# A fused encoder block on one core: the large SBUF tiles moved to multiples of 2 KiB

## The chip, the core and the metric

The kernel runs on one core of a Trainium2 chip. The metric is the device time of one execution in microseconds. TensorE is written PE, its weight loads PEld; VectorE is DVE, ScalarE is ACT, GpSimd is POOL, and SP is the engine whose queue issues most of the DMAs.

## What is computed

One residual block of an encoder on x of 256 rows by 2048 columns, float32, with all weights streamed from HBM once:

```python
h      = rmsnorm(x, g_mix)
proj   = h @ w_in                       # 2048 x 10240: q,k,v twice, two gates
y_sb   = stick_breaking_attention(...)  # 8 heads of 128
y_ca   = chunked_relpos_attention(...)  # 8 heads of 128
x = x + (sigmoid(gate_sb) * (y_sb @ w_sb_out)
         + sigmoid(gate_ca) * (y_ca @ w_ca_out)) @ w_mix_out
h = rmsnorm(x, g_ffn);  g, u = split(h @ w_ffn_in)      # 2048 x 11264
x = x + (silu(g) * u) @ w_ffn_out                       # 5632 x 2048
h = rmsnorm(x, g_ple)
x = x + sigmoid(h @ w_ple_gate) * (p @ w_ple_in)
out = rmsnorm(x, g_final)
```

## The kernel before

**Splitting.** Each float32 operand of a product is split into a rounded part (hi) and a remainder (lo), both float32r, and a product takes three partial products: hi·hi, hi·lo, lo·hi. A piece of 512 KB of weights lands in one of five `raw` buffers; ACT rounds it into `hi` (L173) and DVE subtracts into `lo` (L174), each of three buffers. The activations lie split as well, in tables `T1`, `T2` and `T3` of shape [128, 16, 2, 256]: for each of 16 blocks of the contraction, 256 columns hi and 256 columns lo, 2 KiB in a row.

**Two kinds of product.** A "feat" piece holds four contraction blocks of 256 weight columns. For each block and each half of the columns PE loads 128 columns of `hi` and streams all 512 columns of the table (hi and lo, L198), then loads 128 columns of `lo` and streams the 256 hi columns (L200). I call these two matmuls, 512 and 256 columns, a *pair*. A "row" piece holds two contraction blocks of 512 weight columns; there the table is loaded as weights and 512 columns of `hi` or `lo` are streamed, three matmuls for each block and row half (L181 to L183). In each pair the weights and the streamed table are two different SBUF tiles:

```python
    nc.tensor.matmul(ps, hi[:, i, f], lhs[:, kt, :, :].rearrange("p c s -> p (c s)"),
                     start=a, stop=False)                                        # L198
    nc.tensor.matmul(ps[:, :S], lo[:, i, f], lhs[:, kt, 0, :], start=False, stop=z)  # L200
```

The first argument after the output is loaded as weights, the second is streamed; in `row_products` it is the table that is loaded.

**Stages in order of time.** v of the first four heads and p @ w_ple_in as row pieces (to 51 us, the second with the small table `pT`); then q, k and v of both mixers with the attention worked in between, and both gates, all on T1 (to 504 us); w_sb_out and w_ca_out on T2 (to 594 us); w_mix_out on T1 (to 685 us); then three blocks of w_ffn_in on T3 followed by w_ffn_out on T2, T1 and T2 (T3: 685 to 864, 955 to 1133 and 1224 to 1358 us; T2: 865 to 955 us; T1: 1134 to 1224 us; T2: from 1358 us); last w_ple_gate as row pieces with T1 as weights, its last 512 columns kept split in T2 and T3, and the final norm.

**Order of work.** A list of pieces is worked in order; loads are issued five pieces ahead by SP (L158), splits two ahead, and small tasks (attention, norms) run between pieces. The framework then schedules the instructions of each engine and puts in the semaphores.

**Where the tiles lie.** A pool's tiles lie one behind the other in the order of their first use, each rounded up to 32 bytes, and pools lie behind each other in the order in which they are opened. The offset of a tile in a partition, modulo 2048, before the change: the framework's own constants take the first 128 bytes, so T1, T2 (32 KiB each) and xT (16 KiB) lie at 128. The small constants after them take 4640 bytes (ident 512, ones 512, mhalf 32, gT 192, rbc 1024, three rstd 96, sqs 2048, three ms 96, msq 64, rest 32, rfin 32), so all that follows lies 4640 bytes further, at 672: `raw`, `hi`, `lo` (4 KiB a buffer), v, qT and kT, and T3, which later takes the place of v. A block of 128 weight columns is 512 bytes, so weights out of `hi` and `lo` start at 160 modulo 512, streamed slices of T1 and T2 at 128 and those of T3 at 160. In row pieces the weights out of T1 start at 128 modulo 512, those out of pT (at 1696) at 160, and the streamed `hi` and `lo` at 160. All these numbers are read from the program's allocation.

Of the kernel before, what the change touches and what calls it, by code (L numbers as in the profile page):

```python
# [9 lines left out]
F32 = mybir.dt.float32  # L10
F32R = mybir.dt.float32r
# [5 lines left out]
P = 128  # L17
S = 256
NT = 2
D = 2048  # L20
KD = D // P
# [19 lines left out]
def block_kernel(ctx: ExitStack, tc: tile.TileContext, x, p, w_in, w_sb_out, w_ca_out, w_mix_out,  # L41
# [12 lines left out]
    outr = out[0].rearrange("(t p) d -> p t d", p=P)  # L54

    cp = ctx.enter_context(tc.tile_pool(name="const", bufs=1))
    wp = ctx.enter_context(tc.tile_pool(name="wts", bufs=1))
    dp = ctx.enter_context(tc.tile_pool(name="dram", bufs=1, space=bass.MemoryType.DRAM))
    ps_mm = ctx.enter_context(tc.tile_pool(name="ps_mm", bufs=4, space=PSUM))
# [7 lines left out]
    def const(name, shape, dt=F32):  # L67
        return cp.tile(shape, dt, tag=name, name=name)

    T1 = const("T1", [P, KD, 2, S], F32R)  # L70
    T2 = const("T2", [P, KD, 2, S], F32R)
    xT = const("xT", [P, KD, S])


    ident = const("ident", [P, P])
# [50 lines left out]
    def group(kind, wsrc, n0, kts, lhs, post, needs=lambda kt: None, row0=0, keep=None):  # L126

        ncol, nk = (NB, 2) if kind == "row" else (FB, 4)
        g = dict(kind=kind, post=post, lhs=lhs, ps=None, keep=keep)
        kts = list(kts)  # L130
        for j in range(0, len(kts), nk):
            part = kts[j : j + nk]
            r = (row0 + j) * P
            pieces.append(dict(
                g=g, kts=part, ncol=ncol, first=j == 0, last=j + nk >= len(kts),
                src=wsrc[r : r + len(part) * P, n0 : n0 + ncol].rearrange("(k p) n -> p k n", p=P),
                needs=[k for k in (needs(kt) for kt in part) if k is not None],
            ))
# [78 lines left out]
    def flush(every=1):  # L217

        while state["at"] < len(pieces):
            pc = pieces[state["at"]]  # L220
            prefetch()
            products(pc)
            state["at"] += 1
            if tasks and state["at"] % every == 0:
                run_task()
# [40 lines left out]
    def x_tiles(kt, ps):  # L266
# [5 lines left out]
        for k in range(n):  # L272
            g = gT[:, kt + k : kt + k + 1]
            hi = T1[:, kt + k, 0, :]
            if k == 0:
                nc.scalar.activation(hi, ps[:, k, :], AF.Identity, scale=g)
            else:
                nc.vector.tensor_scalar(hi, ps[:, k, :], g, None, ALU.mult)
            nc.vector.scalar_tensor_tensor(T1[:, kt + k, 1, :], ps[:, k, :], g, hi.bitcast(F32),
                                           ALU.mult, ALU.subtract)  # L280
# [40 lines left out]
    def v_tile():  # L321
        return mp.tile([P, NT, NB], F32, tag="v", name="v")

    def scale_v(v, ps):
        for t in range(NT):
            nc.scalar.activation(v[:, t, :], ps[t], AF.Identity, scale=rstd["mix"][:, t : t + 1])
# [12 lines left out]
    v0 = v_tile()  # L339
    group("row", w2, 2 * W, range(KD), T1, lambda ps: tasks.append(("v", lambda: scale_v(v0, ps))), needs=hneed)  # L340
    for c in range(4):
# [40 lines left out]
    def feat_post(dst, h0, sc, then):  # L382
        def post(ps):
            for f in range(2):
                sm = halves(ps[f], mp)
                if sc is None:
                    nc.vector.tensor_tensor(dst[:, h0 + f, :], sm, rbc, ALU.mult)
                else:
                    nc.vector.scalar_tensor_tensor(dst[:, h0 + f, :], sm, sc, rbc, ALU.mult, ALU.mult)
            if then is not None:  # L390
                then()
        return post

    def split_y(ps, kt):
        src = ps[:, :512].rearrange("p (k s) -> p k s", k=2)
        nc.scalar.copy(T2[:, kt : kt + 2, 0, :], src)
        nc.vector.tensor_tensor(T2[:, kt : kt + 2, 1, :], src, T2.bitcast(F32)[:, kt : kt + 2, 0, :], ALU.subtract)
        done.add(("y", kt))
# [133 lines left out]
    def push_attention(s1, s2, s3):  # L532
        for s, h in ((s1, 0), (s2, 0), (s3, 0), (s1, 2), (s2, 2), (s3, 2)):
            tasks.append((None, lambda s=s, h=h: s(h)))

    for mixer, make in ((0, sb_tasks), (1, ca_tasks)):
        for b in range(2):
# [5 lines left out]
            if not first:  # L543
                group("row", w2, c0 + 2 * W, range(KD), T1, lambda ps, v=v: scale_v(v, ps), needs=hneed)
            for dst, off, sc in ((qT, 0, SCALE), (kT, W, None)):
                for j in range(2):
                    then = None
                    if off and j == 1:
                        then = lambda t=make(qT, kT, v, 4 * b): push_attention(*t)
                    group("feat", w2, c0 + off + j * FB, range(KD), T1, feat_post(dst, 2 * j, sc, then), needs=hneed)  # L550
            flush(4)

    def gate_post(m, j):
        def post(ps):
            for f in range(2):
                sm = halves(ps[f], mp)
                nc.vector.tensor_tensor(gates[:, m, 2 * j + f, :], sm, rbc, ALU.mult)
        return post

    for j in range(8):  # L560
        for m in range(2):
            group("feat", w2, 6 * W + m * D + j * FB, range(KD), T1, gate_post(m, j), needs=hneed)
    flush(4)

    def out_post(m, j):
        def post(ps):
            gt = gates[:, m, 2 * j : 2 * j + 2, :]
            nc.scalar.activation(gt, gt, AF.Sigmoid)
            for f in range(2):
                kt = 2 * j + f  # L570
                sm = halves(ps[f], mp)
                nc.vector.tensor_tensor(gates[:, m, kt, :], sm, gates[:, m, kt, :], ALU.mult)
            if m == 1:
                for kt in (2 * j, 2 * j + 1):
                    mg = gates[:, 0, kt, :]
                    nc.gpsimd.tensor_tensor(mg, mg, gates[:, 1, kt, :], ALU.add)  # L576
                    put_split(T1, kt, mg)
        return post

    for j in range(8):  # L580
        for m, wo in ((0, w_sb_out), (1, w_ca_out)):
            group("feat", wo[0], j * FB, range(8 * m, 8 * m + 8), T2, out_post(m, j),
                  needs=lambda kt: ("y", kt))
# [65 lines left out]
    for blk, nk in enumerate(FF_BLOCKS):  # L649
        dst = (T2, T1, T2)[blk]  # L650
        for i in range(0, nk, 2):
# [73 lines left out]

    keep = [t.rearrange("p k c s -> p (k c s)") for t in (T2, T3)]

# [44 lines left out]
```

## Time and profile before

| | us |
|---|---|
| median of 3 runs | 1529.45 (1529.27 to 1530.86) |
| the profiled execution | 1530.86 |
| its span, first to last instruction | 1529.2 |
| PE busy in the span | 1512.1 |

"PE busy" is the time in which at least one matmul is under way. Matmuls overlap in the profile (each is shown until its results are out), so the pace of PE is read from the distance of two starts and not from a matmul's duration.

### The profile page before, as it was taken

To read this page: it belongs to the slowest core of one execution; us is meant where nothing else is said; L and a number is where in the kernel's file an instruction comes from. 1 tells how busy PE (TensorE), PEld (TensorE's weight loads), DVE (VectorE), ACT (ScalarE), POOL (GpSimd) and SP (SyncE) were. 2 spreads that over 40 slices of the span, in tenths; PEclk is the share of its full clock that TensorE was granted. 3 is DMA by queue.
4 is the path that set the end of the run, shared out by engine and by line. 5 is a ranking of instruction groups with operands and counts; after the bars stand their busy time and mean duration, and the time that the engine had idled before them with its cause. 6 is when DMAs were issued, how large, how long until landed. Compare 5 with 4: busy or idle time off the path is not lost.

```text
span 1529.2 us, 21785 instructions
## 1 busy us (share of the span) xinstructions
PE 1512.1 (99%) x8454; PEld 1307.7 (86%) x8454; DVE 993.6 (65%) x1361; ACT 735.5 (48%) x1001; POOL 131.5 (9%) x118
## 2 busy tenths in 40 slices
PE   8999999999999999999999999999999999999997
PEld 6888888888888888888888888888888888888886
DVE  7566666666555777676666655666665566668575
ACT  5455554555444455454444433444443344445542
POOL 6300000000000122111000000000000000001100
PEclk9999999999999999999999999999999999999999
DMA  8775556555565556656565555656655566655563
GB/s 267 254 222 165 171 173 180 179 174 171 182 190 184 187 187 202 227 185 185 187 193 185 188 192 181 192 186 187 192 188 185 186 187 192 185 184 194 167 215 116
DMA packets 265174, 289.27 MB, mean 189 GB/s; under 512 B 9040, under 2 KB 244864, under 8 KB 264816
## 3 DMA queue, kind: packets, MB, share of 16 engines
q1 hardware_dynamic: 262912, 278.96, 57.7%
q0 software_dynamic: 2160, 8.93, 1.8%
q8 instruction: 66, 1.08, 0.3%
q14 instruction: 36, 0.29, 0.1%
HBM read 282.09 MB, written 5.77 MB: 188 GB/s over the span
## 4 chain that ended last, share of the span: by engine, by line
PE 96%; POOL 1%; DMA 1%; issue 1%; DVE 0%; ACT 0%; SPq 0%; POOLq 0%; DVEq 0%; ACTq 0%
PE mm L198 56%; PE mm L200 28%; PE mm L181 3%; PE mm L182 3%; PE mm L183 3%; DMA raw<-in_w_in 1%; POOL sqs L94 1%; POOL sq L292 1%; PE x2p L672 0%; PE yp L430 0%; PE wt L521 0%; PE zp L421 0%; PE yp L421 0%; PE yp L420 0%; PE zp L419 0%
## 5 line engine op out<-in xcount | busy, mean ns | idle before, releaser
L198 PE MATMUL mm<-T,hi 128*128 128x512 f32 x3648 | 1277.0, 396 | 0.0
L200 PE MATMUL mm<-T,lo 128*128 128x256 f32 x3648 | 1006.6, 280 | 0.0
L174 DVE TENSOR_TENSOR lo<-raw,hi 128x1024 fp32r<-128x1024 f32 (+1 forms) x517 | 642.4, 1243 | 416.6 <-ACT hi L173 411.1
L173 ACT CAST hi<-raw 128x1024 fp32r<-128x1024 f32 (+1 forms) x517 | 541.5, 1048 | 584.3 <-PE mm L198 435.1
L198 PEld LDWEIGHTS mm<-T,hi 128*128 128x128 f32 x3648 | 677.8, 188 | 156.0
L200 PEld LDWEIGHTS mm<-T,lo 128*128 128x128 f32 x3648 | 686.9, 188 | 8.8
L231 ACT COPY tm<-mm 128x256 f32<-128x256 f32 x184 | 68.7, 373 | 125.6 <-PE mm L200 125.6
L233 DVE TENSOR_TENSOR sm<-mm,tm 128x256 f32<-128x256 f32 x184 | 77.3, 420 | 53.9 <-ACT tm L231 53.9
L634 POOL TENSOR_TENSOR tg<-tg,sg 128x512 f32<-128x512 f32 x22 | 39.6, 1800 | 619.4 <-ACT sg L633 619.4
L182 PE MATMUL mm<-lo,T 128*128 128x512 f32 x224 | 88.9, 400 | 0.0
L183 PE MATMUL mm<-hi,T 128*128 128x512 f32 x224 | 87.7, 398 | 0.0
L181 PE MATMUL mm<-hi,T 128*128 128x512 f32 x224 | 84.5, 403 | 0.0
L182 PEld LDWEIGHTS mm<-lo,T 128*128 128x128 f32 x224 | 42.2, 189 | 9.8 <-DVE lo L174 0.4
L181 PEld LDWEIGHTS mm<-hi,T 128*128 128x128 f32 x224 | 42.2, 190 | 9.7
L183 PEld LDWEIGHTS mm<-hi,T 128*128 128x128 f32 x224 | 42.1, 189 | 9.8
L576 POOL TENSOR_TENSOR gates<-gates 128x256 f32<-128x256 f32 x16 | 19.9, 1246 | 291.2 <-ACT hi L173 280.7
L94 POOL TENSOR_TENSOR sqs<-sqs,sq 128x512 f32<-128x512 f32 x21 | 30.9, 1473 | 117.6 <-ACT sq L613 117.3
L607 DVE TENSOR_TENSOR xT<-mm,xT 128x256 f32<-128x256 f32 x64 | 25.0, 424 | 10.9 <-PE mm L200 10.9
L243 DVE SCALAR_TENSOR_TENSOR T<-xT,gT,T 128x256 fp32r<-128x256 f32 x32 | 29.4, 958 | 0.0
L608 DVE TENSOR_TENSOR xT<-mm,xT 128x256 f32<-128x256 f32 x64 | 23.9, 415 | 0.0
L489 POOL DMA_DIRECT2D bias<-ext_d x8 | 4.3, 541 | 200.8 <-DVE sl L414 161.2
L643 DVE TENSOR_TENSOR sm<-sm,rbc 128x256 f32<-128x256 f32 x44 | 18.7, 425 | 1.5
(172 smaller groups left out, 629.9 us busy)
## 6 DMA issues: line engine op xcount, KB each, us to landing
raw<-in_w_ffn_in SPq DMA_DIRECT2D x176, 512.0 KB, 3.5
raw<-in_w_in SPq DMA_DIRECT2D x159, 512.0 KB, 3.6
raw<-in_w_ffn_out SPq DMA_DIRECT2D x88, 512.0 KB, 3.4
raw<-in_w_mix_out SPq DMA_DIRECT2D x32, 512.0 KB, 3.4
raw<-in_w_ple_gate SPq DMA_DIRECT2D x32, 512.0 KB, 4.2
raw<-in_w_sb_out SPq DMA_DIRECT2D x16, 512.0 KB, 3.3
raw<-in_w_ca_out SPq DMA_DIRECT2D x16, 512.0 KB, 3.4
raw<-in_w_ple_in SPq DMA_DIRECT2D x4, 512.0 KB, 5.0
```

The costliest lines, as they stand in the source:

```text
L94: nc.gpsimd.tensor_tensor(sqs, sqs, sq, ALU.add)
L173: nc.scalar.copy(hi[:, c : c + m], raw[:, c : c + m])
L174: nc.vector.tensor_tensor(lo[:, c : c + m], raw[:, c : c + m], hi.bitcast(F32)[:, c : c + m], ALU.subtract)
L181: nc.tensor.matmul(ps, xh, hi, start=a, stop=False)
L182: nc.tensor.matmul(ps, xh, lo, start=False, stop=False)
L183: nc.tensor.matmul(ps, xl, hi, start=False, stop=z)
L198: nc.tensor.matmul(ps, hi[:, i, f], lhs[:, kt, :, :].rearrange("p c s -> p (c s)"), start=a, stop=False)
L200: nc.tensor.matmul(ps[:, :S], lo[:, i, f], lhs[:, kt, 0, :], start=False, stop=z)
L231: nc.scalar.copy(tm, ps[:, S:])
L233: nc.vector.tensor_tensor(sm, ps[:, :S], tm, ALU.add)
L243: nc.vector.scalar_tensor_tensor(dst[:, kt, 1, :], src, g, dst.bitcast(F32)[:, kt, 0, :], ALU.mult, ALU.subtract)
L634: nc.gpsimd.tensor_tensor(tg, tg, sg, ALU.mult)
```

## The change

It opens a pool `big` behind the pool of constants and moves T1, T2 and xT into it; the constants, now first, get an unused tile `fill` of 344 floats (1376 bytes) ahead of them. 128 + 1376 + 4640 = 6144 = 3 · 2048, so T1, T2 and xT lie at multiples of 2 KiB, and with them everything behind: `raw`, `hi`, `lo`, v, qT, kT and T3 move from 672 to 0 modulo 2048, pT to 1024. No instruction is added, removed or changed in its operands' shapes.

```diff
     cp = ctx.enter_context(tc.tile_pool(name="const", bufs=1))
+    bp = ctx.enter_context(tc.tile_pool(name="big", bufs=1))
     wp = ctx.enter_context(tc.tile_pool(name="wts", bufs=1))
...
-    T1 = const("T1", [P, KD, 2, S], F32R)
-    T2 = const("T2", [P, KD, 2, S], F32R)
-    xT = const("xT", [P, KD, S])
+
+    const("fill", [P, 344])
+    T1 = bp.tile([P, KD, 2, S], F32R, tag="T1", name="T1")
+    T2 = bp.tile([P, KD, 2, S], F32R, tag="T2", name="T2")
+    xT = bp.tile([P, KD, S], F32, tag="xT", name="xT")
```

## Rows read from the trace of the kernel before

**Rows 1.** The page: its first line, PE's busy time with its share and count of instructions, the granted clock in 40 slices (9 is 90% or more of full speed), and the chain of work that ended last by engine.
```profile
span 1529.2 us, 21785 instructions
...
PE 1512.1 (99%) x8454; PEld 1307.7 (86%) x8454; DVE 993.6 (65%) x1361; ACT 735.5 (48%) x1001; POOL 131.5 (9%) x118
...
PEclk9999999999999999999999999999999999999999
...
PE 96%; POOL 1%; DMA 1%; issue 1%; DVE 0%; ACT 0%; SPq 0%; POOLq 0%; DVEq 0%; ACTq 0%
```

**Rows 2.** What PE waited for, from the view of the waits of PE: us in total, times, longest.
```profile
PE gps L263 <- DMA gm<-in_g_mix: 3.5, 1, 3.5
PE nps L102 <- POOL sqs L99: 2.4, 1, 2.4
PE xps L271 <- DMA xt<-in_x: 2.0, 1, 2.0
```

**Rows 3.** The largest groups of PE by shape: count, busy us, mean ns of one.
```profile
L198 PE MATMUL mm<-T,hi 128*128 128x512 f32 x3648 | 1277.0, 396 | 0.0
L200 PE MATMUL mm<-T,lo 128*128 128x256 f32 x3648 | 1006.6, 280 | 0.0
L182 PE MATMUL mm<-lo,T 128*128 128x512 f32 x224 | 88.9, 400 | 0.0
L183 PE MATMUL mm<-hi,T 128*128 128x512 f32 x224 | 87.7, 398 | 0.0
L181 PE MATMUL mm<-hi,T 128*128 128x512 f32 x224 | 84.5, 403 | 0.0
L181 PE MATMUL mm<-hi,pT 128*128 128x512 f32 x16 | 7.0, 435 | 0.0
```

**Rows 4.** Line 198 in six stretches, one row for each: count of matmuls, duration min/median/max, and the us in which the first and the last one started. In order: gates on T1, w_sb_out and w_ca_out on T2, w_mix_out on T1, and w_ffn_out on T2, T1 and T2.
```profile
L198 PE MATMUL mm<-T,hi x349: 392/395/402, 380.7 to 503.6; 128*128 128x512 f32 x175
...
L198 PE MATMUL mm<-T,hi x256: 392/397/402, 503.9 to 594.0; 128*128 128x512 f32 x128
...
L198 PE MATMUL mm<-T,hi x256: 392/396/402, 594.4 to 684.5; 128*128 128x512 f32 x128
...
L198 PE MATMUL mm<-T,hi x256: 389/392/402, 864.7 to 954.6; 128*128 128x512 f32 x128
...
L198 PE MATMUL mm<-T,hi x255: 392/395/402, 1134.2 to 1224.0; 128*128 128x512 f32 x128
...
L198 PE MATMUL mm<-T,hi x191: 389/392/402, 1358.8 to 1425.8; 128*128 128x512 f32 x191
```

**Rows 5.** The same for the three blocks of w_ffn_in, on T3.
```profile
L198 PE MATMUL mm<-T,hi x512: 390/395/403, 684.8 to 864.3; 128*128 128x512 f32 x171
...
L198 PE MATMUL mm<-T,hi x512: 391/395/403, 955.0 to 1133.5; 128*128 128x512 f32 x171
...
L198 PE MATMUL mm<-T,hi x384: 391/395/403, 1224.3 to 1358.1; 128*128 128x512 f32 x192
```

**Rows 6.** The timeline of PE in two stretches on T3, the first and the last L198 of each: start us, duration us. Between the first two rows lie 30 pairs, and 30 between the last two.
```profile
770.22 0.40 PE L198 MATMUL mm<-T,hi 128*128 128x512 f32 x1
...
780.62 0.40 PE L198 MATMUL mm<-T,hi 128*128 128x512 f32 x1
...
792.45 0.40 PE L198 MATMUL mm<-T,hi 128*128 128x512 f32 x1
...
803.05 0.40 PE L198 MATMUL mm<-T,hi 128*128 128x512 f32 x1
```

**Rows 7.** The timeline of PE where w_ffn_out on T2 ends and w_ffn_in on T3 begins; the matmul at 954.98 is the first on T3. Between the first two rows lie 15 pairs, between the last two 29.
```profile
949.32 0.39 PE L198 MATMUL mm<-T,hi 128*128 128x512 f32 x1
...
954.62 0.40 PE L198 MATMUL mm<-T,hi 128*128 128x512 f32 x1
...
954.98 0.40 PE L198 MATMUL mm<-T,hi 128*128 128x512 f32 x1
...
955.68 0.39 PE L198 MATMUL mm<-T,hi 128*128 128x512 f32 x1
...
965.74 0.39 PE L198 MATMUL mm<-T,hi 128*128 128x512 f32 x1
```

**Rows 8.** The timeline of PE in two stretches of row pieces: with pT as weights (20 matmuls from the first to the second row) and with T1 as weights (30 from the third to the fourth).
```profile
46.66 0.39 PE L181 MATMUL mm<-hi,pT 128*128 128x512 f32 x1
...
51.19 0.39 PE L183 MATMUL mm<-hi,pT 128*128 128x512 f32 x1
...
1470.17 0.39 PE L182 MATMUL mm<-lo,T 128*128 128x512 f32 x1
...
1477.17 0.39 PE L182 MATMUL mm<-lo,T 128*128 128x512 f32 x1
```

**Rows 9.** The split of the weights by shape on DVE and ACT, into `lo` and `hi` and, for the last pieces, into T2 and T3 (count, busy us, mean ns, idle before); and the issues of the w_ffn_in loads (KB each, median us to landing).
```profile
L174 DVE TENSOR_TENSOR lo<-raw,hi 128x1024 fp32r<-128x1024 f32 x515 | 641.1, 1245 | 415.2 <-ACT hi L173 409.8
...
L174 DVE TENSOR_TENSOR T<-raw,T 128x1024 fp32r<-128x1024 f32 x8 | 9.8, 1224 | 4.1 <-ACT T L173 3.8
...
L173 ACT CAST hi<-raw 128x1024 fp32r<-128x1024 f32 x515 | 540.3, 1050 | 583.0 <-PE mm L198 435.1 <-issue 85.0 <-PE mm L183 49.0
...
L173 ACT CAST T<-raw 128x1024 fp32r<-128x1024 f32 x8 | 8.4, 1052 | 5.7 <-DMA raw<-in_w_ple_gate 5.7
...
raw<-in_w_ffn_in SPq DMA_DIRECT2D x176, 512.0 KB, 3.5
```

## The prediction

> **What bounds the kernel now.** I began with the page. PE is busy for 1512.1 us of a span of 1529.2, the granted clock is at nine tenths or more in all 40 slices, and the chain that ended last is 96% PE [rows 1]. The view of waits names three short ones, 7.9 us in all, at the start and at the first norm [rows 2]; the rest of the 17.1 us without PE is the end after the last matmul. So the time is the number of matmuls times the distance at which PE starts them. The duration column of the groups (396 and 280 ns for 512 and 256 columns, [rows 3]) doesn't give that distance, because matmuls overlap; starts do.
>
> I therefore read first and last starts. On T1 and T2 the six stretches give (503.6 − 380.7)/348 = 353.2 ns a pair, then 353.3, 353.3, 352.5, 353.5 and 352.6 [rows 4]: 353.1 over the 1,557 distances. The three blocks on T3 give 351.3, 349.3 and 349.3 [rows 5]; the first has the norm's matmuls inside, so I take 349.3. Same shapes, same weight buffers, same line of code: only the streamed table differs.
>
> The timeline shows why 349.3 is no pace but a mean. One stretch of 30 pairs on T3 takes 10.40 us, 346.7 ns a pair, another 10.60 us, 353.3 ns [rows 6]. So there is a fast pace and a slow pace, 6.6 ns apart. T3 changes between them and is fast for about 60% of its pairs ((353.3 − 349.3)/6.6); T1 and T2 are slow nearly always. Where the streamed table changes from T2 to T3, with weights out of the same buffers, the pace goes from 353.3 (15 pairs in 5.30 us) to 346.9 (29 in 10.06 us) within two pairs [rows 7]. The row pieces show two paces too: 20 matmuls with pT as weights in 4.53 us, 226.5 ns each, 30 with T1 as weights in 7.00 us, 233.3 ns [rows 8]; the streamed buffers are the same.
>
> **What I take from it.** The program's addresses sort these cases. Streamed T1 and T2 stand at 128 modulo 512 and the weights at 160: 32 bytes apart, slow. T3 and weights both at 160: fast for the larger part. T1 as weights at 128, streamed `hi` at 160: apart, slow. pT at 160, `hi` at 160: fast. So I take it that PE keeps the fast pace when the weights that it loads and the columns that it streams start at the same offset, and that it falls into the slow one when they are 32 bytes apart. The rows show the two paces and where each stands; that the offset is the cause is my reading, and four pairs of tiles are few.
>
> **The change part by part.**
>
> *The pool and the fill.* They add no instruction, no wait and no DMA; `fill` is never read or written. Price nothing. If the framework should order the instructions otherwise, it would show as another sequence on PE.
>
> *T1 and T2 come level with the weights.* After the change both stand at 0 modulo 512: they are related as T3 and the weights are now. In the six stretches 1,563 pairs go from 353.1 to T3's 349.3: 1,563 × 3.8 ns = 5.9 us. Of T1's and T2's 2,240 pairs 677 lie before 381 us, mixed with attention; their pace can't be read off first and last starts, so the bounds are nothing and the same 3.8 ns, 2.6 us. I take half, 1.3 us.
>
> *T3.* It moves together with the weights; their distance stays. Price nothing; bounds: all fast, 1,408 × (349.3 − 346.7) = 3.7 us gained, or all slow, 1,408 × (353.3 − 349.3) = 5.6 us lost.
>
> *Row pieces.* 672 matmuls (3 × 224, [rows 3]) now have T1 32 bytes from `hi`; after it they stand as pT does. Bounds: nothing, or 672 × (233.3 − 226.5) = 4.6 us. pT's stretch is short and T3 keeps the fast pace only for 60%, so I take half, 2.3 us.
>
> *All other tiles.* `raw` is written by DMA, read by ACT and DVE, and its loads land in 3.5 us, issued five pieces (some 14 us) ahead. The splits take 1.05 and 1.24 us of a piece's 2.8 us (eight pairs). The one pair of rows with the same operation at another offset differs little: DVE 1245 ns into `lo` at 672 and 1224 into T2 and T3, ACT 1050 and 1052 [rows 9]. What hides these edits is PE itself; where it doesn't, in the 17.1 us without PE, 2% of it is 0.3 us either way. Price nothing.
>
> Sum: 5.9 + 1.3 + 2.3 = 9.5 us gained. The profiled execution took 1530.86 us, 1.7 over its span and the longest of the three; it would come to 1521.4, the median of 1529.45 to 1520.
>
> [...] Two starts on the same line are 6.6 ns apart where only the table differs [rows 6, 7]. [...]
>
> **The rivals.**
>
> *All fast.* Level tiles could hold the fast pace throughout, also in the long stretches on T1 and T2, which run 250 pairs without a break and so keep whatever pace they were entered with. Then 1,563 × (353.1 − 346.7) = 10.0 us, the early pairs up to 4.3, T3 3.7 and row pieces 4.6: 22.6 us, 1507. For it: pT's 20 matmuls are all fast. Against it: T3 is level today and slow for 40%.
>
> *No effect of addresses.* The two paces may come from the order of the matmuls and the moment at which a stretch begins; that T1 and T2 begin slow would be chance. Then the sequence repeats and the time is 1529.4. For it: T3 at one and the same offset has both paces, and T1 begins at 380.7 us with a stretch behind attention that is no different in kind. Against it: rows 7, where the table alone changes and the pace with it, and both cases of row pieces.
>
> *Slower.* The offset itself may matter and not the distance: T1 and T2, at multiples of 64, are slow in the rows as streamed tables and T1 as weights too; the fast cases have both tiles at 32 past a multiple of 64. After the change all stand at such multiples. Then T3 loses its fast part, 1,408 × 4.0 ns = 5.6 us, and pT's 48 matmuls (three groups of 16, [rows 3]) 0.3: 1535.4. The last 512 columns, where T1 (128) meets T2 (128) and T3 (160), could decide, but they mix both cases in every three matmuls. It decides once T3's share of fast pairs falls from 60% to under 28% while T1 and T2 stay as they are: 1,408 × 0.32 × 6.6 ns = 3.0 us.
>
> *The change doesn't do what it says.* A further constant that I overlooked would put T1 elsewhere by 32 bytes; the distance of T1 to the weights would still be that of two tiles in neighbouring pools, both multiples of 2 KiB long, so level. Small.
>
> **How the numbers follow.** I give the forecast 0.45, all fast 0.13, no effect 0.20, slower 0.20, the change not doing what it says 0.02. Executions agree within some 0.1%, so 0.2%, 3 us, is about what a measurement of this kernel can tell from no change. Faster holds the first two: 0.58. Same holds no effect and the last, 0.22; slower is 0.20. The predicted time is 1520. Its own range is 1514 (the early pairs and row pieces at their upper bounds, with some more of the long stretches fast) to 1526 (no row pieces, no early pairs, a third of the long stretches left slow as they are). The range of all cases goes from all fast, 1507, to T3 slow, 1535; some 0.05 lie under and 0.1 over it.
>
> **What would show it.** In the profile after: the first and last starts of the stretches on T1 and T2 (w_sb_out, w_mix_out, w_ffn_out) divided by their count, 349.3 or less instead of 353.1; T3's as before; row pieces under w_ple_gate at 226.5 to 230 instead of 233.3. The durations on line 198 would lose their 402 ns maximum in fast stretches (the median on T3 is 395, [rows 5]). PE's busy time would fall by what the span falls, DVE, ACT and DMA keep their sums. The prediction is wrong if T1's and T2's stretches stay at 353 (no effect), if T3's go to 353 as well (slower), or if a third pace appears that no row here shows: then the two prices of 346.7 and 353.3 are no bounds.

## The result, and the profile after

The changed kernel took 1521.12 us (median of 5 runs, 1519.61 to 1521.88) beside 1529.45 for the kernel before in the same comparison; the ratio is 0.9942, 95% interval 0.993 to 0.9953. That is faster by 0.58%, and the forecast of 1520 lies 1.1 us under it. The order of the matmuls is the same as before. The change adds three lines of code ahead of them, so line 198 is now 201, 200 is 203, 181 to 183 are 184 to 186, and the splits on 173 and 174 are 176 and 177. The profiled executions took 1530.86 us before and 1521.23 after; the one before lies 1.4 us over its median, so traces show a gain of 9.6 us where the medians show 8.3.

The page after, as [rows 1]: span, busy time of the engines, granted clock in 40 slices, and the chain that ended last by engine.
```profile
span 1519.5 us, 21785 instructions
...
PE 1502.3 (99%) x8454; PEld 1303.0 (86%) x8454; DVE 991.9 (65%) x1361; ACT 735.0 (48%) x1001; POOL 129.6 (9%) x118
...
PEclk9999999999999999999999999999999999999999
...
PE 96%; POOL 1%; issue 1%; DVE 1%; DMA 0%; SPq 0%; ACT 0%; POOLq 0%; DVEq 0%
```
The span is 9.7 us shorter and PE's busy time 9.8 us; DVE, ACT and POOL keep theirs within 2 us, and the mean granted clock is 0.997 in both. So the same matmuls start closer together. By stages, the view of line 201 after (count, duration min/median/max, first and last start), in order of time: w_sb_out and w_ca_out on T2, w_mix_out on T1, a block on T3, w_ffn_out on T2, T3, T1, T3, T2. The rows of T1 and T2 answer to [rows 4] from its second row on, those of T3 to [rows 5].
```profile
L201 PE MATMUL mm<-T,hi x256: 392/394/396, 500.9 to 589.3; 128*128 128x512 f32 x128
...
L201 PE MATMUL mm<-T,hi x256: 392/398/403, 589.6 to 679.6; 128*128 128x512 f32 x128
...
L201 PE MATMUL mm<-T,hi x512: 390/395/403, 679.9 to 859.6; 128*128 128x512 f32 x171
...
L201 PE MATMUL mm<-T,hi x256: 392/395/403, 859.9 to 948.4; 128*128 128x512 f32 x128
...
L201 PE MATMUL mm<-T,hi x512: 392/395/403, 948.7 to 1127.5; 128*128 128x512 f32 x171
...
L201 PE MATMUL mm<-T,hi x256: 392/395/403, 1127.8 to 1216.3; 128*128 128x512 f32 x128
...
L201 PE MATMUL mm<-T,hi x384: 392/395/403, 1216.6 to 1350.6; 128*128 128x512 f32 x192
...
L201 PE MATMUL mm<-T,hi x191: 389/396/403, 1351.3 to 1418.1; 128*128 128x512 f32 x191
```
The T2 stretch of w_sb_out and w_ca_out takes (589.3 − 500.9)/255 = 346.7 ns a pair where it took 353.3; w_ffn_out on T2 and on T1 346.9 each. But w_mix_out on T1 stays at 352.9, and the three blocks on T3 lie at 351.5, 349.9 and 349.8 beside 351.3, 349.3 and 349.3 in [rows 5]. Starts in these views are rounded to 0.1 us; here and below a pace comes from the unrounded starts where the two differ. Two rows of the timeline after, 36 row matmuls apart, with T1 as weights, answer to [rows 8]:
```profile
1461.99 0.39 PE L184 MATMUL mm<-hi,T 128*128 128x512 f32 x1
...
1470.15 0.39 PE L184 MATMUL mm<-hi,T 128*128 128x512 f32 x1
```
8.16 us / 36 = 226.7 ns each, where it was 233.3.

Since both programs issue the same matmuls in the same order, the two traces can be subtracted matmul by matmul. The distance to the next start, before minus after, summed: row pieces up to 51 us 0.2, and from there to 381 us 1.6; pairs up to 381 us 0.1, all else up to there −0.1; the six stretches on T1 and T2 6.3 (1.15, 1.71, 0.11, 1.53, 1.64, 0.15); the three blocks on T3 −0.5; the last row pieces 1.9. That is 9.5 of the 9.7 us; the rest lies ahead of the first matmul and behind the last.

**Why a level stretch has two paces.** A stretch on T3 from 720 us ("x2" are two matmuls of one kind in a row):
```profile
720.68 0.40 PE L201 MATMUL mm<-T,hi 128*128 128x512 f32 x1
...
730.74 0.39 PE L201 MATMUL mm<-T,hi 128*128 128x512 f32 x1
...
731.08 0.63 PE L201 MATMUL mm<-T,hi 128*128 128x512 f32 x2
731.55 0.40 PE L203 MATMUL mm<-T,lo 128*128 128x256 f32 x2
731.78 0.40 PE L201 MATMUL mm<-T,hi 128*128 128x512 f32 x1
...
733.55 0.40 PE L201 MATMUL mm<-T,hi 128*128 128x512 f32 x1
...
733.90 0.63 PE L201 MATMUL mm<-T,hi 128*128 128x512 f32 x2
...
734.60 0.40 PE L201 MATMUL mm<-T,hi 128*128 128x512 f32 x1
...
741.88 0.39 PE L201 MATMUL mm<-T,hi 128*128 128x512 f32 x1
...
742.22 0.63 PE L201 MATMUL mm<-T,hi 128*128 128x512 f32 x2
...
742.92 0.40 PE L201 MATMUL mm<-T,hi 128*128 128x512 f32 x1
...
753.17 0.40 PE L201 MATMUL mm<-T,hi 128*128 128x512 f32 x1
```
29 pairs at 346.9 ns (10.06/29), 5 at 354 (1.77/5), 21 at 346.7 (7.28/21), 29 at 353.4 (10.25/29). Between them stands each time what I call a *swap*: where the scheduler lets two 512-column matmuls follow each other and then two of 256 columns, in place of the strict alternation. In the T3 blocks after, the pace changes at 58 of 59 swaps; before, where T3 and the weights were level as well, at 56 of 59. On T1 before, 32 bytes from the weights, 23 of 24 swaps leave the slow pace as it is. So level tiles don't have one pace with an accidental mixture: they have two, 346.7 and 353.3 ns, and all but 4 of these 118 swaps on T3 turned one into the other.

Tiles 32 bytes apart ran at the fast pace as well, but a swap took it from them and no swap brought it back. Before the change w_ffn_out on T2 began behind a fast end of T3:
```profile
864.66 0.39 PE L198 MATMUL mm<-T,hi 128*128 128x512 f32 x1
...
870.21 0.63 PE L198 MATMUL mm<-T,hi 128*128 128x512 f32 x2
```
Its first 16 pairs take 5.55 us, 346.9 ns each. The swap at 870.4 ends that, and the stretch is slow to its end. Of 30 swaps on T1 and T2 before, three turn fast into slow, 27 stay slow, and none turns slow into fast. So the offset between these tiles is no fixed price of each pair: it decides what a swap does to the pace (58 of 59 turn it at level tiles on T3, 3 of 30 at 32 bytes).

After the change w_mix_out shows what one swap at level tiles costs: it is entered fast at 589.6, has one swap, at 595.2, and its 238 pairs behind it run at 353.3. The two stretches of w_ffn_out have two swaps each, 6 pairs apart, and so leave as fast as they came.

### The profile page after: what moved, and what is told of

Read it like the earlier page. It is cut to its first block, busy times and chain, and to the rows that moved or that the text cites. A ratio compares the mean times of both kernels' runs of the same rounds, so it can differ in the third digit from the quotient of the medians.

```text
span 1519.5 us, 21785 instructions
## 1 busy us (share of the span) xinstructions
PE 1502.3 (99%) x8454; PEld 1303.0 (86%) x8454; DVE 991.9 (65%) x1361; ACT 735.0 (48%) x1001; POOL 129.6 (9%) x118
## 4 chain that ended last, share of the span: by engine, by line
PE 96%; POOL 1%; issue 1%; DVE 1%; DMA 0%; SPq 0%; ACT 0%; POOLq 0%; DVEq 0%
PE mm L201 56%; PE mm L203 28%; PE mm L184 3%; PE mm L185 3%; PE mm L186 3%; POOL sqs L97 1%; POOL sq L295 1%; DMA raw<-in_w_in 0%; DVE lo L177 0%; PE x2p L675 0%; PE yp L433 0%; PE wt L524 0%; PE zp L424 0%; PE zp L423 0%; PE zp L422 0%
```

## The experiments

Offsets are in bytes modulo 512 unless said otherwise. Where an expectation below quotes 349.8 ns, that is a mean over stretches with swaps inside and no pace of its own; starts between two swaps show 346.7 and 353.3. All the kernels of the whole block (experiments 1 to 3, 6, 7 and 10 to 12) issue the same 8,454 matmuls in the same order as the kernel before.

**1. All tiles level, 32 bytes higher.** Same change, `fill` of 352 floats: everything large at 32 modulo 2048.
```diff
-    const("fill", [P, 344])
+    const("fill", [P, 352])
```


> The changed kernel with fill 32 bytes longer: T1, T2, xT, raw, hi, lo and T3 all at 32 modulo 2048, so still level with each other but at no multiple of 64. If the distance between weights and streamed tile is what counts: the time of the changed kernel, 1521 us, T1's and T2's long stretches at 346.7 ns a pair and row pieces at 227. If the place itself counts (multiples of 64 or 2 KiB): about 1529 us, T1's and T2's stretches at 353 and row pieces at 233.

1520.67 us, ratio 0.9937 (0.9924 to 0.9949): the gain of the change without its multiples of 2 KiB. The T2 stretch and w_mix_out (here and below each row holds also the last matmul of the stage before, so 256 distances):
```profile
L201 PE MATMUL mm<-T,hi x257: 392/392/395, 498.8 to 587.6; 128*128 128x512 f32 x129
...
L201 PE MATMUL mm<-T,hi x257: 392/398/403, 587.6 to 677.9; 128*128 128x512 f32 x129
```
The eight stages from 500 us have the paces of after to the last digit (346.7, 352.9, 351.5, 346.9, 349.9, 346.9, 349.8, 351.7), the last long stretch of row pieces is at 227.2 in both. So the place itself, modulo 64 or 2 KiB, isn't what counts between these two layouts (1521.12 and 1520.67 us).

**2 and 3. The weights moved away again.** The change, and an unused tile behind xT: 32 bytes in one kernel, 64 in the other. T1 and T2 stay at multiples of 2 KiB; weights and T3 stand 32 (64) bytes behind.
```diff
     xT = bp.tile([P, KD, S], F32, tag="xT", name="xT")
+    bp.tile([P, 8], F32, tag="pad", name="pad")      # 16 in the other
```


> The changed kernel with 32 unused bytes behind xT: T1, T2 and xT stay at multiples of 2 KiB, raw, hi, lo and T3 stand at 32. If the distance counts: T1's and T2's stretches fall back to about 353 ns a pair and row pieces to 233, T3 stays near 349.8: 1529 to 1531 us. If the place of T1 and T2 at multiples of 2 KiB counts: 1521 us as in the changed kernel.

> The changed kernel with 64 unused bytes behind xT: weights and T3 at 64, T1 and T2 at multiples of 2 KiB. If only the half of a 64-byte line counts, in which both start: as the changed kernel, 1521 us, row pieces at 227. If weights and table must start at the same offset modulo 512 or 2048: about 1529 us, row pieces at 233.

1529.36 us, ratio 0.9996 (0.9987 to 1.0005), and 1528.82, 0.9992 (0.9983 to 1.0001): the whole gain is gone in both. The T2 stretch and w_mix_out with 32 bytes, then with 64:
```profile
L202 PE MATMUL mm<-T,hi x257: 392/392/402, 502.0 to 592.4; 128*128 128x512 f32 x129
...
L202 PE MATMUL mm<-T,hi x257: 392/395/402, 592.4 to 682.9; 128*128 128x512 f32 x129
```
```profile
L202 PE MATMUL mm<-T,hi x257: 397/397/398, 501.7 to 592.2; 128*128 128x512 f32 x129
...
L202 PE MATMUL mm<-T,hi x257: 388/397/398, 592.2 to 682.6; 128*128 128x512 f32 x129
```
90.4 to 90.5 us for 256, 353.3 ns a pair, in all four, and at 64 bytes all 24 swaps on T1 leave it so. Row pieces are at 233.2 with 32 bytes; with 64 they are at 229.1, where 233 was expected. Together with experiment 1 this shows the distance of weights and streamed table as the cause: the same 32 bytes change nothing if all tiles take them and everything if the weights alone do. In experiments 1 and 2 `hi`, `lo` and T3 have the very same addresses, and yet T3's mean is 349.9 in the one and 349.4 in the other: its swaps are the same, the pace with which it is entered isn't.

**4 and 5. Offsets measured by themselves.** Two kernels that compute nothing of the block: they only stream matmuls of both kinds from three tiles, at chosen offsets. The first runs 12 combinations four times, the second 20 offsets of the weights once in rising and once in falling order. The heart of it:
```python
# "row":  32 times
nc.tensor.matmul(ps[t], wh[:, w : w + P], mv[:, a : a + 512], start=first, stop=last)
# "feat": 16 pairs
nc.tensor.matmul(ps[t], wh[:, w : w + P], mv[:, a : a + 512], start=first, stop=False)
nc.tensor.matmul(ps[t][:, :S], wl[:, v : v + P], mv[:, a : a + S], start=False, stop=last)
```


> Matmuls alone: no block is computed, only streams of the kernel's two kinds of product out of copies of x, 12 combinations of streamed start and weight start (bytes modulo 512), each four times, 32 matmuls of a row piece and 16 pairs of a feat piece a time. If the distance counts: (0,0), (32,32), (16,16) and (160,160) at 226.7 ns a row matmul and 346.7 a pair, (0,32), (32,0) and (128,160) at 233.3 and 353.3; (0,64), (0,128), (0,256) tell the modulus, (0,8) and (0,16) how fine it is. If the place counts, (32,32) and (160,160) differ from (0,0). If neither counts and the pace is a matter of how a stream is entered, every combination shows the same mix.

> Matmuls alone again, no block is computed: the streamed operand starts at 0, the weights at 20 offsets from 0 to 504 bytes behind it, each as 32 row matmuls and as 16 pairs, once with the offsets rising and once falling; then pairs with hi and lo at different offsets, and level pairs entered behind 1 to 8 small matmuls, which change the moment of entry alone. Distance theory: row matmuls show 226.7 ns at few distances (0 and about 256) and 233.3 at the others whatever came before; pairs at 0 show 346.7 or 353.3 depending on the entry, and there are distances at which every entry gives 346.7 (16 in the first map). Rival, that only the way of entry counts: rising and falling order and the number of small matmuls move every distance's pace alike.

From the second kernel, ns of a matmul ("row") and of a pair, streamed columns at 0, by the weights' offset (12 of the 20); two values where the two orders differ by more than 1:

| weights at | 0 | 16 | 32 | 64 | 96 | 128 | 192 | 256 | 320 | 448 | 480 | 496 |
|---|---|---|---|---|---|---|---|---|---|---|---|---|
| row | 226.7 | 233.3 | 233.3 | 233.3 | 234.4 | 232/233 | 228.9 | 226.7 | 233.3 | 228.9 | 233.3 | 228.3 |
| pair | 353.3 | 346.7 | 353.3 | 353.3 | 346.7 | 351.1 | 353.3 | 347/353 | 353.3 | 349/353 | 346.7 | 353/347 |

Row matmuls agree with the kernel before and after: 226.7 at 0 and 256, 233.3 at 32. In the first kernel, by (streamed columns, weights), (32, 32) and (160, 160) are at 226.7 to 227.6 and (0, 32), (32, 0) and (128, 160) at 233.3. Experiment 3 fits too: there the weights lie 448 past the streamed `hi`, for which the table has 228.9. Two expectations failed in the first kernel. (16, 16) is level, but its row matmuls ran at 231 or 233.3 and its pairs always at 346.7; and pairs at (32, 0) ran at 346.7 where (0, 32) ran at 353.3. Pairs don't follow the two-pace picture that I had: level tiles come out slow here (at (160, 160) fast or slow by the order), 16 bytes fast. In the second kernel a small matmul of 64 columns was scheduled into the level streams after every 19; its timeline, tiles level at 0:
```profile
591.37 0.20 PE L51 MATMUL lead<-mv,wh 128*128 128x64 f32 x1
...
591.83 0.40 PE L62 MATMUL mm<-mv,wh 128*128 128x512 f32 x1
...
594.61 0.39 PE L62 MATMUL mm<-mv,wh 128*128 128x512 f32 x1
594.84 0.19 PE L51 MATMUL lead<-mv,wh 128*128 128x64 f32 x1
...
595.07 0.39 PE L62 MATMUL mm<-mv,wh 128*128 128x512 f32 x1
...
597.90 0.40 PE L62 MATMUL mm<-mv,wh 128*128 128x512 f32 x1
```
Eight pairs in 2.78 us (347.5 ns) after the first small matmul, eight in 2.83 (353.8) after the second, over and over. At 16 bytes the stretches between small matmuls all settle at 346.7. So here too a break turns the pace where the tiles are level, and there is a distance at which it doesn't.

**6. Sixteen bytes, by moving the tables.** T1, T2 and T3 at 16, `hi` and `lo` at 32. The excerpt shows T1 and T2; T3 becomes the part from 496 bytes on of a tile that is 512 bytes longer.
```diff
-    T1 = bp.tile([P, KD, 2, S], F32R, tag="T1", name="T1")
-    T2 = bp.tile([P, KD, 2, S], F32R, tag="T2", name="T2")
+    N_T = KD * 2 * S
+    T12 = bp.tile([P, 2 * N_T + 8], F32R, tag="T12", name="T12")
+    T1, T2 = (T12[:, 4 + i * N_T : 4 + (i + 1) * N_T].rearrange("p (k c s) -> p k c s", k=KD, c=2)
+              for i in range(2))
```


> The changed kernel with T1, T2 and T3 placed so that hi and lo stand 16 bytes behind them modulo 512 (T at 16, weights at 32). If the distance sets the pace and 16 bytes give the fast one from any entry, as the map has it: the stretches on T1, T2 and T3 all at 347 ns a pair, T3 from 349.8 too, row pieces (T1 16 bytes ahead of hi) at about 228.3 where they had 227.2. 3,648 pairs at 347 instead of 349.8 in the mean are 10 us, so about 1511 us. If only the way in which a stretch is entered counts: stretches at two paces as in the changed kernel and 1519 to 1523 us.

1531.99 us, ratio 1.0003 (0.9994 to 1.0012): a miss. T2's stretch, 241 distances in 85.2 us, is at 353.3 ns a pair, and all 59 swaps on T3 leave the slow pace as it is:
```profile
L203 PE MATMUL mm<-T,hi x242: 397/397/398, 506.6 to 591.8; 128*128 128x512 f32 x121
```
**7. The same distance, by moving the weights.** T1, T2 and T3 at 0, `hi` and `lo` at 16, with `fill` of 88 floats. Each of `hi` and `lo` becomes one tile that holds the three buffers.
```diff
+    hi3 = wp.tile([P, 3 * 1024 + 8], F32R, tag="hi", name="hi")
+    lo3 = wp.tile([P, 3 * 1024 + 248], F32R, tag="lo", name="lo")
...
-            hi = wp.tile([P, 1024], F32R, tag="hi", name="hi", bufs=3)[:, :n]
-            lo = wp.tile([P, 1024], F32R, tag="lo", name="lo", bufs=3)[:, :n]
+            c0 = state["split"] % 3 * 1024
+            hi = hi3[:, c0 + 4 : c0 + 4 + n]
+            lo = lo3[:, c0 + 124 : c0 + 124 + n]
```


> The changed kernel with the tables kept at multiples of 512 and hi and lo at 16: the same distance as in the run with the tables at 16 and the weights at 32, but in the places of the map. If the place within 32 bytes counts as well as the distance, pairs run at 347 from any entry and the time is 1509 to 1515 us. If the distance alone counts, the time is that run's, 1531 us. If long stretches in the kernel don't follow the map of short streams, pairs stay at 350 to 353.

1514.18 us, ratio 0.9892 (0.9878 to 0.9906), as expected. The same stretch, 256 distances:
```profile
L204 PE MATMUL mm<-T,hi x257: 392/392/392, 497.9 to 586.7; 128*128 128x512 f32 x129
```
346.7 ns, T3 at 347.5, row pieces at 231.6; all 59 swaps on T3 leave the fast pace as it is. The distance is 16 bytes in both kernels, and one loses 18 us against the other. So beside the distance it matters, within 32 bytes, where the tiles start, as (16, 16) had shown in the streams. Whether it is the start of the tables or that of the weights, these two kernels can't tell: both differ by 16.

**8 and 9. `hi` and `lo` apart.** Two more kernels of streams, with the streamed columns at 0, over 8 x 8 offsets of `hi` and `lo`, then over 16 x 16 in steps of 32.

> Matmuls alone, no block is computed: pairs with the streamed operand at 0 and hi and lo at eight offsets each (0, 16, 32, 48, 64, 448, 480, 496), 64 combinations, each once in rising and once in falling order. If a collision of the load of the next weights with the columns being streamed makes the slow pace, hi and lo count each for itself, the pace falls into rows and columns of the table, and some combinations lie under 346.7 ns (0 with 480 gave 344.4 in the map). If 346.7 is a floor that no place can lower, none lies under it but by entry.

> Matmuls alone, no block is computed: pairs with the streamed operand at 0 and hi and lo each at 16 offsets, the multiples of 32 up to 480, every combination in rising and in falling order, 12 pairs a time. If the pace is set by the two distances, the two orders agree in most of the 256 combinations, (448, 0) is at 340.0 again, level (0, 0) shows 346.7 or 353.3, and there are more combinations at 340 than one; if entry sets it, the two orders disagree at random.

346.7 is no floor. In the first map (hi, lo) = (448, 0) gives 340.0 in both orders and (64, 0) 350 or 340 by order. In the second it is the other way round: (64, 0) and (320, 0) give 340.0 in both orders, (448, 0) and (192, 0) 350 or 340. So streams show both paces at both places, and the maps don't tell which a kernel will get. Nor does the pace fall into one part for `hi` and one for `lo`, as the entry of the first map had it: with `hi` at 64 it is 340.0 for `lo` at 16 and 353.3 for `lo` at 64. The second map repeats every 256 bytes in `hi` (255 of 256 pairs of values within 1.5 ns); at some 200 of its 256 places the two orders agree within 1.5 ns.

**10. `hi` 64 bytes ahead of the tables, `lo` level.** The change, with `fill` of 216 floats and two unused tiles.
```diff
+            if state["split"] == 0:
+                wp.tile([P, 112], F32, tag="pad1", name="pad1")
             hi = wp.tile([P, 1024], F32R, tag="hi", name="hi", bufs=3)[:, :n]
+            if state["split"] == 0:
+                wp.tile([P, 16], F32, tag="pad2", name="pad2")
```


> The changed kernel with hi 64 bytes ahead of the tables (448 modulo 512) and lo level with them, made with two pads among the weight buffers and a shorter fill. In the map of hi and lo this combination ran at 340.0 ns a pair from both entries. If the map carries over to the kernel: T1's, T2's and T3's stretches at 340 to 342, 3,648 pairs 8 to 9 ns faster, row pieces at 228 to 232 (hi 64 ahead of T1, lo level), so 1489 to 1500 us. If the paces of long stretches are set by entry and 346.7 can't be kept under: 1517 to 1525 us.

1492.33 us, ratio 0.9751 (0.9737 to 0.9765), as expected: 38 us under the kernel before, where the change gave 8. First T2, then the last block on T3 (384 distances):
```profile
L205 PE MATMUL mm<-T,hi x257: 389/389/389, 495.2 to 582.3; 128*128 128x512 f32 x129
...
L205 PE MATMUL mm<-T,hi x385: 388/389/398, 1194.2 to 1325.3; 128*128 128x512 f32 x193
```
340.0 and 341.4 ns a pair. The stretches on T1 and T2 from 495 to 1194 us are at 340.0 to 340.3, row pieces at 231.7 to 233.5. After each of the 59 swaps on T3 a few pairs are slower, then 340 is back. One stretch of 16 pairs behind the second norm ran at 350.0.

**11. `hi` 64 bytes behind.** The two pads exchanged (16 and 112 floats).

> The same change as in the kernel with `hi` 64 bytes ahead of the tables, with the two pads exchanged: `hi` starts 64 bytes behind the tables (64 modulo 512), `lo` level with them (0 modulo 512); T1, T2, T3, `raw` as there. In the map of both offsets the pair (64, 0) kept 340.0 ns in both orders, (448, 0) 340.0 or 350. Theory (the signed offset of `hi` modulo 256 counts): pairs 340 on T1 and T2 and at least as steady on T3, where `hi` 64 ahead gave 341.4 to 343.5: some 1,408 x 2 ns = 2.8 us less at most. Row matmuls have T1 as weights 448 behind `hi` (228.9 in the map by offsets) and level with `lo` (226.7): some 228.2 in place of 231.5 to 233.7, 672 x 4 ns = 2.7 us less. So 1487 to 1492 us. Rival (only the size of the gap counts, its sign doesn't): as with `hi` ahead, 1492.3, rows 232. Rival (the fastest pace there was a matter of entry): pairs back to 347 to 353, 1515 to 1525.

1524.32 us, ratio 0.996 (0.9946 to 0.9974): a miss by 32 us; the rival of the entry came true. First T2, then the last block on T3:
```profile
L205 PE MATMUL mm<-T,hi x257: 393/393/396, 501.1 to 590.8; 128*128 128x512 f32 x129
...
L205 PE MATMUL mm<-T,hi x385: 392/393/396, 1218.5 to 1352.8; 128*128 128x512 f32 x193
```
350.0 and 349.7 ns a pair, and all 59 swaps on T3 leave it there. The entry went by the second map, which had 340.0 at this place in both orders; the first map had shown 350.0 there in one of them. In the kernel the stretches are entered at 350 and stay there. Row pieces came out at 232.7, no better than in experiment 10, against what I expected.

**12. The kernel before, with the two pads only.** No pool `big`, no `fill`; T1 and T2 remain at 128, `hi` comes to 64, `lo` and T3 to 128.
```diff
+            if state["split"] == 0:
+                wp.tile([P, 104], F32, tag="pad1", name="pad1")
             hi = wp.tile([P, 1024], F32R, tag="hi", name="hi", bufs=3)[:, :n]
+            if state["split"] == 0:
+                wp.tile([P, 16], F32, tag="pad2", name="pad2")
```


> The kernel before with two unused pads only (416 bytes ahead of `hi`, 64 behind it): no pool `big`, T1 and T2 stay at 128 modulo 512, `raw` at 672 modulo 2048; `hi` comes to 64 modulo 512, `lo` and T3 to 128. So `hi` lies 64 bytes ahead of the tables and `lo` level, as in the kernel of 1492.3 us, but everything 128 modulo 512 higher. Theory (the distances decide, a shift of all tiles by a multiple of 32 bytes changes nothing, as with the level tiles at 32): pairs 340.0 to 340.3 on T1 and T2, 341 to 344 on T3, 1490 to 1496 us. Rival (340 or 350 by how the stretches are entered, as `hi` 64 bytes behind gave 350.0 throughout): 350 in part or in all, 1500 to 1526. Rival (multiples of 2 KiB are a part of it): slower than 1496 with paces other than 340 and 350.

1492.51 us, ratio 0.9756 (0.9743 to 0.9769). Its page, then T2, w_mix_out and the last block on T3:
```profile
span 1489.1 us, 21785 instructions
...
PE 1472.4 (99%) x8454; PEld 1290.7 (87%) x8454; DVE 991.1 (67%) x1361; ACT 735.1 (49%) x1001; POOL 130.3 (9%) x118
...
L202 PE MATMUL mm<-T,hi x257: 389/389/389, 490.8 to 577.8; 128*128 128x512 f32 x129
...
L202 PE MATMUL mm<-T,hi x257: 388/389/398, 577.8 to 664.9; 128*128 128x512 f32 x129
...
L202 PE MATMUL mm<-T,hi x385: 388/389/398, 1189.7 to 1320.7; 128*128 128x512 f32 x193
```
These are 340.0, 340.1 and, on T3, 341.4 ns. The paces by stage are those of experiment 10 to 0.3 ns, from a layout that is shifted by 128 bytes as a whole. Multiples of 2 KiB are no part of this gain (1492.51 us with T1 and T2 at 128).

## Why the prediction was right, and where its terms were off

**The bound and the cause.** That PE's starts alone set the time held: span and PE's busy time fell by the same 9.7 to 9.8 us, matmul by matmul. That the distance between weights and streamed table makes the gain was my reading of four pairs of tiles. Experiments 1 to 3 show it for the offsets in question: moving all tiles another 32 bytes keeps the gain (1520.67 us), moving the weights alone by 32 or 64 takes it away (1529.36 and 1528.82). What I had wrong is how the distance acts. I priced each table at a mean pace of its own; in both kernels a stretch has one of two paces, 346.7 or 353.3 ns, and the distance decides what a swap does to it.

**The sum.** 9.5 us were forecast and the traces show 9.5 between the first and the last matmul. That the sum came out so exactly is luck: by its terms it was 0.4 short on T1 and T2, 1.2 over on the early pairs, 1.4 short on row pieces and 0.5 over on T3.

**T1 and T2, six stretches: 5.9 forecast, 6.3 measured.** Right in size by two errors against each other. I gave every level stretch T3's 349.3 as a mean. There is no such pace: three of the six are fast all but throughout (T2 1.71 us gained, T2 1.53, T1 1.64), the gates change at every swap (1.15), and w_mix_out and the last T2 stretch gain only 0.11 and 0.15, because a swap leaves their longest runs, 238 and 117 pairs, slow. Nor were T1 and T2 slow nearly always before: where they were entered fast, as T2 at 864.7 us, they stayed so up to the next swap. Which stretch is which, I couldn't have read from the sum; the swaps could have been read from the order of lines 198 and 200 in the trace of before.

**Early pairs: 1.3 forecast, 0.1 measured.** The lower bound, all but. In runs of at least six distances between two breaks, up to 381 us, 133 of 571 already had the fast pace before, 32 bytes apart, and 174 of 580 had it after: 41 × 6.6 ns = 0.27 us. Attention breaks the alternation often, and after the change 20 of these 30 level runs still are slow.

**T3: nothing forecast, 0.5 lost.** Inside the bounds. Its distance didn't change, but it is entered at other paces, and its longer stretches fall to the slow side more often: in stretches of six pairs and more 52% of the pairs are fast, where 59% were before.

**Row pieces: 2.3 forecast, 3.7 measured** (0.2 up to 51 us, 1.6 from there to 381, 1.9 at the end). The mis-sized term. I halved the full price of 4.6 because T3 keeps the fast pace for 60%. But that is the swaps' doing, which row pieces don't have in their streams; the rows with T1 as weights run at 227.4 in the mean, near pT's 226.5 [rows 8].

**Everything else: nothing forecast, 0.1 lost up to 381 us and nothing behind it.** DVE's and ACT's splits kept their durations. The page after, with two half pieces in each group (hence "+1 forms"); the same lines of the page before have means of 1243 and 1048:
```profile
L177 DVE TENSOR_TENSOR lo<-raw,hi 128x1024 fp32r<-128x1024 f32 (+1 forms) x517 | 641.3, 1241 | 410.5 <-ACT hi L176 404.8
L176 ACT CAST hi<-raw 128x1024 fp32r<-128x1024 f32 (+1 forms) x517 | 542.2, 1049 | 577.3 <-PE mm L201 435.2
```
**The rivals.** *No effect of addresses* falls with experiments 2 and 3, where tables and order stay, the weights alone move, and the gain goes. Still, half of what spoke for it is true: T3's two paces at one offset do come from the order of the matmuls and the pace of entry (56 of 59 swaps turn one into the other before the change, 58 of 59 after it). *Slower, by the place modulo 64* falls with the result itself and with experiment 1; yet experiments 6 and 7 show that place counts within 32 bytes (1531.99 and 1514.18 us at one distance of 16), which I had not considered. *All fast* was near in its mechanism (up to the next swap a stretch kept its pace: T2's 256 pairs 346.7 ns, w_mix_out's last 238 pairs 353.3) and wrong in its outcome, since at level tiles swaps turn it slow, as the one in w_mix_out did. My line "if a third pace appears, then 346.7 and 353.3 are no bounds" didn't come about in the changed kernel; it did in experiments 10 to 12, at 340.0 (and 350.0 in 11).

**What no run shows.** Experiments 2 and 12 have the same matmuls on the same data and differ only in where the tiles lie: 1529.36 and 1492.51 us, 353.3 and 340.0 ns a pair on T2, so up to 13.3 ns in a pair. What in PE or SBUF makes the difference stays open: no run here looks inside.

**What stays open.** Which event decides between 340 and 350 with `hi` 64 bytes from the tables: ahead of them the long stretches of experiments 10 and 12 ran at 340, behind them those of experiment 11 at 350, while streams alone showed either pace at either place. So that ahead is better than behind is shown for this kernel's order of matmuls only. Nor was it tried to remove the swap in w_mix_out, which by my estimate from its 238 pairs would be worth 238 × 6.6 ns = 1.6 us at level tiles.

## What to carry to other kernels

Where a matmul-bound stage is paced by starts, compare the pace between two starts across pairs of tiles; if equal shapes differ by a few ns, read the tiles' offsets from the allocation before the schedule. Measure the relative offset of weights and streamed operand in the kernel itself, with an unused tile of some tens of bytes: two such tiles were worth 2.4% here (experiment 12), and multiples of 2 KiB as such were worth nothing (experiments 1 and 12). Maps from streams alone only say where to try: of four forecasts made from them, two failed in the kernel (experiments 6 and 11). Distrust a mean pace: here 349.3 was two paces and an order of instructions.

## What the runs showed of the hardware

- A float32r pair of 512 and 256 columns, each with its own weights, ran in long stretches of the kernel at 340.0 (experiments 10 and 12), 346.7 (after the change), 350.0 (experiment 11) or 353.3 ns (before it, experiments 2, 3 and 6), by offsets and entry; a row matmul of 512 columns took 226.7 to 234.4 ns in kernel and streams. No pace below 340.0 was seen to hold, in the kernel or in streams.
- In the streams of experiment 9 the dependence on `hi`'s offset repeats every 256 bytes (255 of 256 pairs of values within 1.5 ns). In this kernel `hi` 64 bytes ahead of the table gives 1492.3 us, 64 behind it 1524.3, level 1521.1; streams show 340 and 350 ns on either side.
- At level tiles one break in the alternation turned 346.7 into 353.3 and the next one back: two matmuls of a kind in a row at 58 of 59 swaps on T3 after the change, one small matmul in the streams of experiment 5 (347.5 and 353.8 ns in turn). At 32 bytes, on T1 and T2 before it, swaps turned 346.7 into 353.3 (three of 30) and never back (none of 30); with `hi` alone 64 bytes ahead (experiment 10), pairs returned to 340.0 after all 59.
- Within 32 bytes the place counts too: weights 16 bytes behind the tables give 1514.2 us with the tables at a multiple of 32 and 1532.0 with them 16 past one; in streams level row matmuls took 226.7 ns at 0, 226.7 to 227.6 at 32 and 160 and 231 to 233.3 at 16.
